# A hybrid encoder layer on one core: other places for evacuated tiles, more steps in the preparation of the scan's time steps, an earlier end of the descending scan, and narrower additions in the last blocks

## The chip, the cores and the metric

The kernel runs on 1 core of one Trainium2 chip. The metric is the device time of one execution in microseconds (us). Before the change the median of 3 runs is 1773.84 us (1771.46 to 1775.32).

Engines are named as in the profile: PE is TensorE (PEld its loading of weights), ACT ScalarE, DVE VectorE, POOL GpSimd, SP SyncE, which issues nearly all DMA transfers of this kernel.

## The reference

One layer of a bidirectional encoder for two request groups with shared weights, 1024 rows and 256 rows, that is 10 tiles of 128 rows:

```python
hn = rms_norm(x, norm_g)
proj = hn @ w_in                       # 2048 -> 4896 columns
xbc, z_ssd, dt_raw, q, k, v, z_att, mq, z_mem = split_cols(proj, IN_SIZES)
xbc = silu(centred_dwconv(xbc, conv_w, conv_b))
dt = softplus(dt_raw + dt_bias)
y = ssd_scan(forward) + ssd_scan(backward) + d_skip * xs
o_ssd = rms_norm(y * silu(z_ssd), ssd_norm_g)            # 1024 columns, two groups
o_att = window_attention(q, k, v, sink) * silu(z_att)    # 512 columns
o_mem = softmax_attention(mq, mem) * silu(z_mem)         # 512 columns
return x + concat([o_ssd, o_att, o_mem]) @ w_out
```

Everything is float32. `ssd_scan` is a chunked state-space scan in chunks of 128 rows; its weights are exponentials of cumulative sums of dt, and the kernel works with logarithms of dt.

## The kernel before, in words

Every weight product is done with split operands: a float32 matrix is split into a high and a low part (`wh`, `wl` for weights, `xH`, `xL` for activations), and three matmuls (`wh*xH`, `wl*xH`, `wh*xL`) stand for one. `wh` is made by ACT (L216), `wl` by DVE (L217), `xH` by ACT (L200) and `xL` by DVE (L201), the last two from a loaded tile `chd` of 128x640. The program runs through three parts: projection blocks whose features are worked through in pairs (L1316 to L1318), ordinary projection blocks (tokens by features, L268 to L270, and features by tokens, L303 to L305), and the output product, first two column blocks by L268 to L270, then eight units of pairs (`block_pair` with `ev_pair`), which end the program. PE's accumulators are five PSUM buffers (`acc`); all other products share three PSUM buffers (`mix`).

Beside the blocks of the projections and of the output product run two lanes of generators. After each step of a block, `pump` takes so many steps from each lane as the rates say; a step ends where the generator has a `yield`. Lane 0 has attention (`attn`, `mem_attn`), lane 1 the scan: `dt_prep` (time steps, cumulative sums and logarithms for one group of five tiles), `ssd_up` (ascending direction, tiles 0 to 9) and `ssd_down` (descending, tiles 7 to 0, then 9 and 8). So a `yield` more or less moves all later steps of a lane against the matmuls of the block. The framework then orders each engine's queue by priorities, and each engine works through its own queue in order.

The places that the change touches:

- `ev_gate` (L315) and `ev_raw` (L335) take a finished accumulator of a q, mq, z0 or z1 block to memory: ACT writes it into a tile of the pool `ev`, tag `evu` for even i and `evt` for odd i, two buffers each, and SP stores it (L342). A block of five tiles has i = 0 to 4. `base` is 0 for the first group of tiles and 5 for the second. The tag `ch` (four buffers of 128x640, `CH` = 4) is that of the loads `chd` and of the rows `yt` to which the output is added.
- `dt_prep` (L568): after the cumulative sums (`pacs`, copied to `ac` by ACT, L612) two rounds of Newton's method for the logarithm (ACT L614, DVE L616 to L620), then two exponentials (L621, L622), and, behind a `yield`, two transposes `pact` on PE (L629, L630), whose copy `acT` is stored.
- `ssd_up` (L876) pauses for some lane steps after its loads: 6 in tile 0, 8 in tile 4, otherwise 3.
- `ssd_down` (L1091): for tiles 0 and 8 (the last of each descending run) it pauses, calls `norm_ssd` (DVE L1074, scales `yd` by `yrs`, which POOL makes) and `turn_ssd` for both groups: four transposes `pr` each on PE (L647, the line of a helper), a copy `so` on ACT (L1088) and a store `oT<-so` on SP (L1089). For tile 0 the output product's first two column blocks wait for these stores: the last chd loads of the activations (`chd<-oT`, L188) read what they write.
- `mem_attn`, which runs beside this end: `pms` (scores, PE L811 to L813), row maxima `mm` (DVE L815), `mpr` (exponentials, ACT L821), `pmt` (transposes, PE L647), `mpT` (ACT L839), `pmo` (PE L850). Of `ssd_up` for tile 8: `pcb` (PE L893), `cb` (ACT L900), `pxs` (PE L930), `xs` and `xf` (DVE), `fh` (ACT L952), `pst` (PE L937).
- `ev_pair` (L1232) adds, for the eight units of the end, the seven products of a pair (p is the product's number) to two rows of tiles `r0` and `r1`, 128x640 each as two halves of 320; every `add` is DVE's L1240. `r0` is stored whole at p = 3 (L1256), `r1` in halves at p = 7 (L1259) and p = 4 (L1262), in this order at the end.

Of the kernel before, what the change touches and what calls it, by code (L numbers as in the profile page):

```python
# [19 lines left out]
P = 128  # L20
# [24 lines left out]
def hymba_encoder_kernel(  # L45
# [80 lines left out]
    def hv(ap, n=8):  # L126
        return ap.rearrange("p (h d) -> p h d", h=n)
# [184 lines left out]
            evac(1, ps[1])  # L312


    def ev_gate(c, base):  # L315
        def f(i, ps):
            z = ev.tile([P, 512], F32, tag="evt" if i % 2 else "evu", name="zs")
            A.activation(z, ps, AF.Tanh, scale=0.5)
            V.scalar_tensor_tensor(out=z, in0=z, scalar=1.0, in1=ps, op0=ALU.add, op1=ALU.mult)
            S.dma_start(z_d[c][base + i], z)  # L320
        return f
# [12 lines left out]

    def ev_raw(dst, base):  # L335
        def f(i, ps):
            if base == 0 and i > 2:
                z = fin.tile([P, 512], F32, tag="tH7" if i == 4 else "tL7", name="qs")
            else:
                z = ev.tile([P, 512], F32, tag="evt" if i % 2 else "evu", name="qs")  # L340
            last_raw[0] = A.activation(z, ps, AF.Copy).ins
            S.dma_start(dst[base + i], z)  # L342
        return f
# [224 lines left out]
    def dt_prep(t0):  # L568
        grp = t0 // 5
        ts = slice(t0, t0 + 5)  # L570
        flat = lambda a: a[:, ts, :].rearrange("p t h -> p (t h)")
        t6 = (t0 + 1) % 6
        wj, dd = [a[:, t6:t6 + 5, :].rearrange("p t h -> p (t h)") for a in (wj_all, dd_all)]
        t5 = lambda a: a.rearrange("p (t h) -> p t h", t=5)
        x = flat(dt_all)
        e, s = [mp.tile([P, 512], F32, tag="xs", name=n, bufs=2)[:, :160] for n in "es"]
        w, l = [mp.tile([P, 512], F32, tag=f"ya{i}", name=n, bufs=1)[:, :160] for i, n in enumerate("wl")]
        V.scalar_tensor_tensor(out=e, in0=x, scalar=-1.0, in1=x, op0=ALU.mult, op1=ALU.min)
        A.activation(e, e, AF.Exp)
        V.tensor_scalar(out=s, in0=e, scalar1=2.0, scalar2=None, op0=ALU.add)  # L580
        V.reciprocal(out=s, in_=s)
        V.tensor_mul(s, s, e)
        V.tensor_mul(w, s, s)
        V.tensor_scalar(out=e, in0=w, scalar1=1.0 / 17, scalar2=None, op0=ALU.mult)
        for c in (15, 13, 11, 9, 7, 5, 3):
            V.scalar_tensor_tensor(out=e, in0=e, scalar=1.0 / c, in1=w, op0=ALU.add, op1=ALU.mult)
        V.scalar_tensor_tensor(out=e, in0=e, scalar=1.0, in1=s, op0=ALU.add, op1=ALU.mult)
        V.tensor_scalar(out=e, in0=e, scalar1=2.0, scalar2=None, op0=ALU.mult)
        V.scalar_tensor_tensor(out=x, in0=x, scalar=0.0, in1=e, op0=ALU.max, op1=ALU.add)
        yield  # L590

        da = e
        V.tensor_mul(t5(da), dt_all[:, ts, :], aneg.unsqueeze(1).broadcast_to([P, 5, 32]))
        yield

        V.tensor_scalar(out=w, in0=x, scalar1=1e-30, scalar2=None, op0=ALU.max)
        V.tensor_scalar(out=l, in0=w.bitcast(I32), scalar1=math.log(2.0) / 2 ** 23, scalar2=-126.957 * math.log(2.0),
                        op0=ALU.mult, op1=ALU.add)
        yield
        yield  # L600
        lower = w2("lower")[:, :P]
        G.affine_select(out=lower, in_=ones, compare_op=ALU.is_ge, fill=0.0, base=0,
                        pattern=[[-1, P]], channel_multiplier=1)
        yield
        yield
        ps = psum("pacs")
        p5 = t5(ps[:, :160])
        T.matmul(p5[:, :, 0:16], upper, t5(da)[:, :, 0:16], start=True, stop=True)
        T.matmul(p5[:, :, 16:32], lower, t5(da)[:, :, 16:32], start=True, stop=True)
        T.matmul(ps[:, 160:320], ones, da, start=True, stop=True)  # L610
        ac = wb("ac", shape=(P, 512))
        A.activation(ac[:, :320], ps[:, :320], AF.Copy)  # L612
        for _ in range(2):
            A.activation(s, l, AF.Exp)  # L614
            d = da
            V.tensor_sub(d, w, s)  # L616
            V.tensor_add(s, w, s)
            V.reciprocal(out=s, in_=s)
            V.tensor_mul(d, d, s)
            V.scalar_tensor_tensor(out=l, in0=d, scalar=2.0, in1=l, op0=ALU.mult, op1=ALU.add)  # L620
        A.activation(flat(eacs_all), ac[:, 0:160], AF.Exp)  # L621
        A.activation(flat(cd_all), ac[:, 160:320], AF.Exp)  # L622
        V.tensor_sub(wj, l, ac[:, 0:160])
        V.tensor_add(dd, wj, ac[:, 160:320])
        A.activation(dd, dd, AF.Exp)
        V.tensor_sub(t5(wj)[:, :, 16:32], t5(wj)[:, :, 16:32], t5(wj)[:, :, 0:16])
        yield
        ps = psum("pact")
        T.transpose(ps[:, :P], ac[:, 0:128], ident)  # L629
        T.transpose(ps[:32, P:2 * P], ac[:, 128:160], ident)  # L630
        acT = wb("acT", shape=(P, 512))
        A.activation(acT[:, :P], ps[:, :P], AF.Copy)
        A.activation(acT[:32, P:2 * P], ps[:32, P:2 * P], AF.Copy)
        S.dma_start(ac_d[grp][0:P, :], acT[:, :P])
        S.dma_start(ac_d[grp][P:160, :], acT[:32, P:2 * P])
        yield
# [239 lines left out]
    def ssd_up(t):  # L876
# [7 lines left out]
        for g in range(2):  # L884
            x = wb("xc", F32R, shape=(P, 4, P))
            S.dma_start(x.bitcast(F32), xbc_d[4 * g:4 * g + 4, :, tok].rearrange("f p c -> p f c"))
            xc.append(x)
        for _ in range(6 if t == 0 else 8 if t == 4 else 3):
            yield

        ps = psum("pcb")
# [199 lines left out]
    def ssd_down(t):  # L1091
# [66 lines left out]
        last_y["y"] = t, [x[0] for x in ld], rs  # L1158
        yield
        if first:  # L1160
            for _ in range(3):
                yield
            norm_ssd()
            yield
            yield
            for g in range(2):
                turn_ssd(g)
                yield

# [60 lines left out]
    def ev_pair(u):  # L1232
# [6 lines left out]
        def add(out, ps, x):  # L1239
            V.tensor_tensor(out=out, in0=ps, in1=x, op=ALU.add)  # L1240

        def f(p, ps):
            if p == 1:
                A.activation(w[:, 0], ps, AF.Copy)
                add(r0[:, 0], ps, r0[:, 0])
            elif p == 2:
                add(r0[:, 0], ps, r0[:, 0])
            elif p == 6:
                add(w[:, 0], ps, w[:, 0])
            elif p == 5:  # L1250
                add(w[:, 1], ps, w[:, 0])
                add(r0[:, 1], w[:, 1], r0[:, 1])
                add(r1, w, r1)
            elif p == 3:
                add(r0[:, 1], ps, r0[:, 1])
                S.dma_start(hv(y_turned[rows_[0], :], 2), r0)  # L1256
            elif p == 7:
                add(r1, ps.unsqueeze(1).broadcast_to([P, 2, 320]), r1)
                S.dma_start(y_turned[rows_[1], 320:], r1[:, 1])  # L1259
            else:  # L1260
                add(r1[:, 0], ps, r1[:, 0])
                S.dma_start(y_turned[rows_[1], :320], r1[:, 0])  # L1262
# [546 lines left out]
```

## Time and profile before

| what | value |
|---|---|
| median of 3 runs | 1773.84 us |
| the profiled execution's own time | 1773.66 us |
| its span in the trace | 1772.0 us |
| PE's granted clock | 1.000 |
| DMA, mean over the span | 170 GB/s, 301.16 MB |

The span runs from the first instruction to the last; the execution's own time is a little longer. In a row of the timeline stand the start in us, the duration in us, the engine, the line, the operation, the tiles (out<-in), the count, and in brackets how long the engine stood idle before it and what ended that. Matmuls overlap: a 128x512 acc matmul is drawn 0.39 us long, and the next one starts 0.23 us later. SPq rows are issues of transfers and not their duration. In a row of the windows come busy times of PE, PEld, DVE, ACT and POOL with instruction counts, then the granted clock, the DMA share and GB/s.

### The profile page before, as it was taken

The page shows a single profiled execution, that of the slowest core. Times are in us where ns is not written, and L with a number is a line of the kernel's source. Part 1 is how long each engine was busy: PE and PEld are TensorE (multiplying, and loading weights), DVE is VectorE, ACT ScalarE, POOL GpSimd, SP SyncE. Part 2 cuts the span into 40 slices and gives each one's busy share as a digit, 9 for nine tenths or more (in the row PEclk, how much of TensorE's full clock was granted, in tenths as well). Part 3 has the DMA queues.
Part 4 walks back from the last instruction along what each step waited for, and adds up shares of the span by engine and source line. Part 5 has one row for each costly group of instructions (what it writes and reads, how often), then busy time and mean ns, then how long its engine had stood idle before and what let it go on. Part 6 is the DMA issues. An engine that isn't in the chain of part 4 may idle for free. (4 is left out here: it accounts for less than half of the span.)

```text
span 1772.0 us, 31942 instructions
## 1 busy us (share of the span) xinstructions
PE 1762.2 (99%) x11044; PEld 1608.4 (91%) x11044; DVE 1246.0 (70%) x2351; ACT 901.6 (51%) x2010; POOL 555.6 (31%) x980
## 2 busy tenths in 40 slices
PE   9999999999999999999999999999999999999999
PEld 7889999999998999999889988888988888899999
DVE  5596788888868878878665676566776654766665
ACT  6555455554434756656454555544446533543332
POOL 0105899998810100001001000011110000058775
PEclk9999999999999999999999999999999999999999
DMA  9654444445446645454545645557777755744442
GB/s 308 189 182 130 136 151 146 144 140 169 124 140 209 197 134 151 140 153 122 186 121 173 201 149 161 172 161 249 225 246 226 257 188 148 218 142 148 145 144 77
DMA packets 208210, 301.16 MB, mean 170 GB/s; under 512 B 19568, under 2 KB 86192, under 8 KB 208048
## 3 DMA queue, kind: packets, MB, share of 16 engines
q1 hardware_dynamic: 207904, 299.06, 54.1%
q8 instruction: 87, 1.43, 0.3%
q14 instruction: 75, 0.61, 0.1%
q10 hardware_dynamic: 144, 0.06, 0.0%
HBM read 236.36 MB, written 62.69 MB: 169 GB/s over the span
## 5 line engine op out<-in xcount | busy, mean ns | idle before, releaser
L217 DVE TENSOR_TENSOR wl<-wraw,wh 128x512 fp32r<-128x512 f32 (+1 forms) x480 | 346.4, 724 | 238.4 <-ACT wh L216 225.4
L216 ACT ACTIVATE wh<-wraw 128x512 fp32r<-128x512 f32 (+1 forms) x480 | 292.2, 613 | 301.6 <-PE acc L270 154.6
L268 PE MATMUL acc<-wh,xH 128*128 128x512 f32 (+1 forms) x1088 | 418.1, 385 | 0.0
L270 PE MATMUL acc<-wh,xL 128*128 128x512 f32 (+1 forms) x1088 | 410.4, 377 | 0.0
L269 PE MATMUL acc<-wl,xH 128*128 128x512 f32 (+1 forms) x1088 | 409.5, 376 | 0.0
L270 PEld LDWEIGHTS acc<-wh,xL 128*128 128x128 f32 x1088 | 204.2, 188 | 37.0 <-issue 0.2
L268 PEld LDWEIGHTS acc<-wh,xH 128*128 128x128 f32 x1088 | 204.3, 188 | 36.5 <-issue 2.7
L269 PEld LDWEIGHTS acc<-wl,xH 128*128 128x128 f32 x1088 | 204.5, 188 | 35.0 <-issue 1.2
L303 PE MATMUL acc<-xH,wh 128*128 128x320 f32 x640 | 203.0, 317 | 0.0
L305 PE MATMUL acc<-xH,wl 128*128 128x320 f32 x640 | 198.8, 311 | 0.0
L304 PE MATMUL acc<-xL,wh 128*128 128x320 f32 x640 | 198.5, 310 | 0.0
L216 ACT ACTIVATE sh<-ws 128x384 fp32r<-128x384 f32 x176 | 91.4, 523 | 204.8 <-POOL ws L1284 111.2
L217 DVE TENSOR_TENSOR sl<-ws,sh 128x384 fp32r<-128x384 f32 x176 | 124.4, 710 | 98.3 <-ACT sh L216 96.0
L1284 POOL TENSOR_TENSOR ws<-wraw 128x128 f32<-128x128 f32 x176 | 113.8, 646 | 202.4 <-DMA wraw<-in_w_in_pairs_dram 90.5
L303 PEld LDWEIGHTS acc<-xH,wh 128*128 128x128 f32 x640 | 120.1, 188 | 2.9 <-issue 2.4
L304 PEld LDWEIGHTS acc<-xL,wh 128*128 128x128 f32 x640 | 120.2, 188 | 1.7 <-issue 1.4
L305 PEld LDWEIGHTS acc<-xH,wl 128*128 128x128 f32 x640 | 120.2, 188 | 1.0 <-issue 0.9
L1284 POOL TENSOR_TENSOR ws<-wraw,ws 128x128 f32<-128x128 f32 x176 | 116.5, 662 | 13.8
L1284 POOL TENSOR_TENSOR ws<-ws,wraw 128x128 f32<-128x128 f32 x176 | 118.2, 671 | 0.0
L1284 POOL TENSOR_TENSOR wraw<-wraw 128x128 f32<-128x128 f32 x176 | 111.5, 633 | 13.7
L654 POOL MEMSET lgw<- 128x1 f32 x40 | 4.2, 105 | 312.0 <-DVE lg L718 161.6
L377 DVE SCALAR_TENSOR_TENSOR c<-u,vec,c 128x638 f32<-128x638 f32 (+1 forms) x96 | 90.0, 939 | 1.1 <-ACT c L372 0.4
(442 smaller groups left out, 3931.1 us busy)
## 6 DMA issues: line engine op xcount, KB each, us to landing
wraw<-in_w_in_laid_dram SPq DMA_DIRECT2D x176, 256.0 KB, 2.9
wraw<-in_w_in_pairs_dram SPq DMA_DIRECT2D x112, 256.0 KB, 2.7
wraw<-in_w_out_laid_dram SPq DMA_DIRECT2D x64, 256.0 KB, 3.6
wraw<-in_w_out_pairs_dram SPq DMA_DIRECT2D x64, 256.0 KB, 2.7
rf<-ac SPq DMA_DIRECT2D x40, 256.0 KB, 4.0
rb<-ac SPq DMA_DIRECT2D x40, 256.0 KB, 4.7
wraw<-in_w_mem_laid_dram SPq DMA_DIRECT2D x32, 256.0 KB, 4.3
xst<-in_x_sample_dram SPq DMA_DIRECT2D x20, 256.0 KB, 5.3
```

Source lines behind the costliest of these rows:

```text
L216: a = A.activation(h, raw, AF.Copy)
L217: b = V.tensor_sub(l, raw, h.bitcast(F32))
L268: T.matmul(ps[t][:, :n], sh, h[:, :n], start=(k_ == 0), stop=False)
L269: T.matmul(ps[t][:, :n], sh, l[:, :n], start=False, stop=False)
L270: T.matmul(ps[t][:, :n], sl, h[:, :n], start=False, stop=(k_ == KT - 1))
L303: T.matmul(o, sh, cur["H", q][:, m, c], start=(k == 0), stop=False)
L304: T.matmul(o, sh, cur["L", q][:, m, c], start=False, stop=False)
L305: T.matmul(o, sl, cur["H", q][:, m, c], start=False, stop=(k == KT - 1))
L377: V.scalar_tensor_tensor(out=c[0], in0=u[:, k:k + n], scalar=cw[k], in1=c[0], op0=ALU.mult, op1=ALU.add)
L654: G.memset(w.bitcast(F32)[(slice(None),) + tuple(slice(n - 1, n) for n in shape)], 0.0)
L1284: G.tensor_tensor(out=o, in0=x, in1=y, op=op)
```

## The change

1. A helper `out_place` chooses the tile for `ev_gate` and `ev_raw`. For the second group of tiles (`base` 5), i = 3 and i = 4 go to the tag `ch`; for the first group all stays.
2. In `dt_prep` the two exponentials move ahead of the two rounds of the logarithm, and each round ends with a `yield`.
3. The pauses of `ssd_up` for tiles 0 and 4 are two lane steps shorter.
4. In `ssd_down`, for tile 0: the pause ahead of `norm_ssd` is one step shorter, one `yield` behind it goes, and that between the two `turn_ssd` goes.
5. In `ev_pair` the store of `r0` is split in two halves (p = 2 and p = 3), and the addition of `w` to `r1`, 640 wide at p = 5, becomes two of 320 (p = 6 and p = 5).

```diff
+    def out_place(i, base, name):
+
+        if i > 2 and base == 0 and name == "qs":
+            return fin.tile([P, 512], F32, tag="tH7" if i == 4 else "tL7", name=name)
+        if i > 2 and base:
+            return rp.tile([P, 640], F32, tag="ch", name=name, bufs=CH)[:, :512]
+        return ev.tile([P, 512], F32, tag="evt" if i % 2 else "evu", name=name)
...
-            z = ev.tile([P, 512], F32, tag="evt" if i % 2 else "evu", name="zs")
+            z = out_place(i, base, "zs")
...
-            if base == 0 and i > 2:
-                z = fin.tile([P, 512], F32, tag="tH7" if i == 4 else "tL7", name="qs")
-            else:
-                z = ev.tile([P, 512], F32, tag="evt" if i % 2 else "evu", name="qs")
+            z = out_place(i, base, "qs")
...
         A.activation(ac[:, :320], ps[:, :320], AF.Copy)
+        A.activation(flat(eacs_all), ac[:, 0:160], AF.Exp)
+        A.activation(flat(cd_all), ac[:, 160:320], AF.Exp)
         for _ in range(2):
             A.activation(s, l, AF.Exp)
...
             V.scalar_tensor_tensor(out=l, in0=d, scalar=2.0, in1=l, op0=ALU.mult, op1=ALU.add)
-        A.activation(flat(eacs_all), ac[:, 0:160], AF.Exp)
-        A.activation(flat(cd_all), ac[:, 160:320], AF.Exp)
+            yield
...
-        for _ in range(6 if t == 0 else 8 if t == 4 else 3):
+        for _ in range(4 if t == 0 else 6 if t == 4 else 3):
             yield
...
         if first:
-            for _ in range(3):
+            for _ in range(2 if t == 0 else 3):
                 yield
             norm_ssd()
             yield
-            yield
+            if t:
+                yield
             for g in range(2):
                 turn_ssd(g)
-                yield
+                if t or g:
+                    yield
...
             elif p == 2:
                 add(r0[:, 0], ps, r0[:, 0])
+                S.dma_start(y_turned[rows_[0], :320], r0[:, 0])
             elif p == 6:
                 add(w[:, 0], ps, w[:, 0])
+                add(r1[:, 0], w[:, 0], r1[:, 0])
             elif p == 5:
                 add(w[:, 1], ps, w[:, 0])
                 add(r0[:, 1], w[:, 1], r0[:, 1])
-                add(r1, w, r1)
+                add(r1[:, 1], w[:, 1], r1[:, 1])
             elif p == 3:
                 add(r0[:, 1], ps, r0[:, 1])
-                S.dma_start(hv(y_turned[rows_[0], :], 2), r0)
+                S.dma_start(y_turned[rows_[0], 320:], r0[:, 1])
```

What this does to the order of the engines is shown at three places. The first is PE at the end of the descending scan, at about 1318 us of the span. The `acc` matmuls are those of the first output block; the number of an `acc` is that of a tile of 128 rows, five to a round. Before:

```order
L268 MATMUL acc_16123<-wh_16158,xH0_15840 128x512
L269 MATMUL acc_16123<-wl_16159,xH0_15840 128x512
L270 MATMUL acc_16123<-wh_16158,xL0_15841 128x512
L647 MATMUL pr_16179<-identr_84,yw_16177 128x128 x4
L647 MATMUL pr_16189<-identr_84,yw_16187 128x128 x4
L783 MATMUL pmq_16199<-identr_84,mq_16145 128x128 x4
```

And with the change (the helper's line is L653 there, and acc_16121 to acc_16125 are the five tiles):

```order
L268 MATMUL acc_16121<-wh_16178,xH0_15840 128x512
L269 MATMUL acc_16121<-wl_16179,xH0_15840 128x512
L270 MATMUL acc_16121<-wh_16178,xL0_15841 128x512
L653 MATMUL pr_16151<-identr_84,yw_16149 128x128 x4
L653 MATMUL pr_16161<-identr_84,yw_16159 128x128 x4
L268 MATMUL acc_16122<-wh_16178,xH0_15840 128x512
```

The eight transposes stood behind the last of the five tiles of a round and now stand behind the first: 12 matmuls earlier. pmq keeps its place behind the round.

The second is ACT just after it. chd_16197, 16237, 16324 and 16365 are the loads of one stretch of activations, chd_16424 and later ones those of the next. Before:

```order
L796 ACTIVATE mqh_16204<-pmq_16199 128x512
L216 ACTIVATE wh_16403<-wraw_16401 128x512
L821 ACTIVATE mpr_16250,mden_16251<-pms_16240,mm_16247,mr_16153 128x256 x2
L900 ACTIVATE cb_16266<-pcb_16257 128x256
L821 ACTIVATE mpr_16278,mden_16279<-pms_16268,mm_16275,mr_16153 128x256 x2
L200 ACTIVATE xH2_16320<-chd_16197,vec_200 128x640
L200 ACTIVATE xH2_16320<-chd_16237,vec_200 128x640
L216 ACTIVATE wh_16450<-wraw_16448 128x512
L200 ACTIVATE xH2_16320<-chd_16324,vec_200 128x640
L200 ACTIVATE xH2_16320<-chd_16365,vec_200 128x640
L952 ACTIVATE fh_16340<-xf_16338 128x512
```

And with the change; behind the last row shown come one more wh and then fh_16340:

```order
L802 ACTIVATE mqh_16204<-pmq_16199 128x512
L200 ACTIVATE xH2_16320<-chd_16197,vec_200 128x640
L216 ACTIVATE wh_16403<-wraw_16401 128x512
L200 ACTIVATE xH2_16320<-chd_16237,vec_200 128x640
L200 ACTIVATE xH2_16320<-chd_16324,vec_200 128x640
L200 ACTIVATE xH2_16320<-chd_16365,vec_200 128x640
L827 ACTIVATE mpr_16250,mden_16251<-pms_16240,mm_16247,mr_16173 128x256 x2
L906 ACTIVATE cb_16266<-pcb_16257 128x256
L200 ACTIVATE xH3_16505<-chd_16424,vec_200 128x640
L827 ACTIVATE mpr_16278,mden_16279<-pms_16268,mm_16275,mr_16173 128x256 x2
L216 ACTIVATE wh_16450<-wraw_16448 128x512
L200 ACTIVATE xH3_16505<-chd_16471,vec_200 128x640
```

The four xH of the first stretch stood behind both softmax steps (mpr) and now stand ahead of them; the first two of the next stretch stand ahead of fh, behind which they were.

The third is PE in the second `dt_prep`, at about 875 us, beside a step of `mem_attn`. Before:

```order
L647 MATMUL pmt<-identr,mprw 128x128 x4
L629 MATMUL pact<-identr,ac 128x128
L630 MATMUL pact<-identr,ac 32x128
L850 MATMUL pmo<-mpT,mv 128x128 x8
L268 MATMUL acc<-wh,xH_6939 128x512
```

And with the change (lines L653, L856, L635 and L636 there):

```order
L653 MATMUL pmt<-identr,mprw 128x128 x4
L856 MATMUL pmo<-mpT,mv 128x128 x8
L635 MATMUL pact<-identr,ac 128x128
L636 MATMUL pact<-identr,ac 32x128
L268 MATMUL acc<-wh,xH_6939 128x512
```

The two transposes pact stood ahead of pmo and now stand behind it.

## Prediction

> **What bounds the kernel now.** I read the head of the page first, then the list of waits on TensorE, then the timeline of each place that the change touches. The head gives the span and how much of it TensorE is busy:
>
> ```profile
> span 1772.0 us, 31942 instructions
> PE 1762.2 (99%) x11044; PEld 1608.4 (91%) x11044; DVE 1246.0 (70%) x2351; ACT 901.6 (51%) x2010; POOL 555.6 (31%) x980
> ```
>
> TensorE works for 1762.2 of 1772.0 us, and the change leaves its matmuls as they are, so only its waits can be won or lost. All of them, by what ended them (total us, times, longest):
>
> ```profile
> PE warm L1592 <- DVE zero L1590: 1.3, 1, 1.3
> PE pst L937 <- ACT fh L952: 1.1, 1, 1.1
> PE pmt L647 <- DVE mpr L827: 1.1, 1, 1.1
> PE ppt L647 <- ACT pT L734: 1.0, 1, 1.0
> PE pmo L850 <- ACT mpT L839: 0.8, 1, 0.8
> PE pr L647 <- ACT so L1088: 0.4, 1, 0.4
> PE acc L1318 <- DVE wl L217: 0.3, 1, 0.3
> ```
>
> They come to 6.0 us, 0.34% of the span. The edits lie near three of them (ppt, pmo, pst) and at the end of the program, after TensorE's last matmul. So 1.0 + 0.8 + 1.1 us and some tenths at the end are all that can be won; against the 0.2% (3.5 us) that a measurement of this kernel can tell from no change, a gain can hardly be seen. A loss has no such bound.
>
> **The new places for evacuated tiles: -0.95.** TensorE, ScalarE and SyncE where mq is stored:
>
> ```profile
> 1228.12 0.65 PE L647 MATMUL ppt<-identr,lgw 128*128 128x128 f32 x4 [0.95 <-ACT pT L734]
> 1227.20 0.60 ACT L341 ACTIVATE qs<-acc 128x512 f32<-128x512 f32 x1 [1.06 <-DMA mq<-qs]
> 1221.72 1.31 SPq L342 DMA_DIRECT2D mq<-qs  x2
> ```
>
> The fifth evacuation of the mq block (i = 4) stands 1.06 us on ScalarE, since its evu buffer is free only when the store of i = 0, issued at 1221.72, is done. pT is queued behind it on ScalarE, and TensorE waits 0.95 us for pT. With i = 3 and 4 in ch buffers no store is waited for: -0.95. At worst half comes back, if a ch buffer is still being read.
>
> The price is in the same queue. Four chd<-oT loads (320 KB each) for the output blocks, which SyncE issued two projection blocks earlier, now come at 1232 to 1246, because the ch buffers are lent out until then:
>
> ```profile
> 1232.00:1246.00 14.00, 14.00 (x113) 12.71 (x111) 10.18 (x19) 4.96 (x11) 5.46 (x12) 1.00 0.94 294
> ```
>
> The DMA share there is 0.94 already, so some transfers land later, by an estimated 0.4 to 1.1 us. TensorE is busy for all 14 us of that stretch, and the next wait behind it (pr for so, 0.4) hangs on a VectorE chain that doesn't start with these transfers. I take 0, and up to +0.7 if that chain is late.
>
> **A yield in each round of the logarithms: +0.25.** The second dt_prep, on TensorE and ScalarE:
>
> ```profile
> 875.21 0.30 PE L629 MATMUL pact<-identr,ac 128*128 128x128 f32 x1
> 875.46 1.06 PE L850 MATMUL pmo<-mpT,mv 128*128 128x128 f32 x8
> 877.30 1.16 PE L850 MATMUL pmo<-mpT,mv 128*128 128x128 f32 x8 [0.79 <-ACT mpT L839]
> 875.91 0.34 ACT L614 ACTIVATE s<-l 128x160 f32<-128x160 f32 x1 [2.05 <-DVE l L620]
> 876.67 0.58 ACT L839 ACTIVATE mpT<-pmt 128x512 f32<-128x512 f32 x1
> ```
>
> ScalarE stands 2.05 us before s, in order, and mpT comes behind; both keep their places in ScalarE's queue. So pmo still starts at 877.30. But the two pact transposes, which took 875.21 to 875.46 ahead of pmo, now follow it: they lay within the wait and now lie on the path. +0.25, at best 0 (if mpT comes earlier), at most +0.3. In the first dt_prep no wait of TensorE is near, and the scan tiles' pauses, shorter by as many steps as dt_prep has more, leave TensorE's order alone: 0, and what hides them is the matmuls of the projection block.
>
> **The shorter descending end: +1.7.** First the transposes pr, which move ahead of 12 acc matmuls:
>
> ```profile
> 1315.85 0.39 PE L268 MATMUL acc<-wh,xH 128*128 128x512 f32 x1
> 1318.58 0.80 PE L647 MATMUL pr<-identr,yw 128*128 128x128 f32 x8
> 1316.36 0.88 DVE L1074 TENSOR_SCALAR yd<-yd,yrs 128x512 f32<-128x512 f32 x2 [2.16 <-POOL yrs L1157]
> 1316.96 0.49 POOL L1082 MEMSET yw<- 128x1 f32 x2 [0.64 <-DVE yd L1074]
> 1319.36 1.07 ACT L1088 ACTIVATE so<-pr 128x512 f32<-128x512 f32 x2
> ```
>
> The 12 acc take 2.73 us (0.2275 each), so TensorE now reaches pr at 1315.85. Its input, the first half of the yd pair, is ready at about 1316.8 (1317.2 if it needs the memset too): a new wait of 1.1 us (1.0 to 1.4), where there was none. In return the stores oT<-so leave earlier: pr at 1316.95, so from 1317.45 to 1318.0, the store at 1318.05 and not at 1319.97 as in the next rows (the chain of waits, the windows, then the timelines):
>
> ```profile
> 1319.97 4.54 DMA oT<-so
> 1324.90 5.86 DMA chd<-oT
> 1318.00:1322.00 4.00, 4.00 (x27) 3.42 (x26) 1.39 (x2) 2.10 (x4) 0.00 (x0) 1.00 0.94 287
> 1324.53 1.75 SPq L188 DMA_DIRECT2D chd<-oT  x4
> 1325.78 0.57 ACT L821 ACTIVATE mpr<-pms,mm,mr 128x256 f32<-128x256 f32 x1 [1.84 <-DVE mm L817]
> 1328.65 0.83 ACT L200 ACTIVATE xH<-chd,vec 128x640 fp32r<-128x640 f32 x1 [0.31 <-DMA chd<-oT]
> 1330.79 0.83 ACT L200 ACTIVATE xH<-chd,vec 128x640 fp32r<-128x640 f32 x1 [1.29 <-DMA chd<-oT]
> 1331.52 0.61 ACT L216 ACTIVATE wh<-wraw 128x512 fp32r<-128x512 f32 x1
> 1332.04 1.54 ACT L200 ACTIVATE xH<-chd,vec 128x640 fp32r<-128x640 f32 x2
> 1334.10 0.63 ACT L952 ACTIVATE fh<-xf 128x512 fp32r<-128x512 f32 x1 [0.52 <-DVE xf L950]
> 1327.03 0.54 PE L930 MATMUL pxs<-identr,xc 128*128 128x128 f32 x4
> 1334.78 0.50 PE L937 MATMUL pst<-fh,bth 128*128 128x512 f32 x1 [1.09 <-ACT fh L952]
> ```
>
> Before, ScalarE ran the first softmax mpr at 1325.78 and only then came to xH, which waited for the loads. Now four xH stand ahead of the first mpr and two more ahead of fh; each waits for its own chd load, and all that is behind waits with it. Worked through: the store lands 3.6 us after 1318.05 (4.54 before; two wraw loads that lay ahead of it now come after the loads), so the loads are issued from 1321.65. The first is there 4.1 us later (1324.53 to 1328.65), at 1325.8; the fourth between 1328.2 (0.8 apart) and 1329.9 (before, the fourth xH began by 1332.8, 8.3 after the first issue): I take 1329.0. Then xH 0.75 and two mpr, 0.57 each: 1330.9. pxs needs the PSUM buffer that mpr frees (three serve all of these tiles); it stands 5 acc later than before and behind the pr wait, at 1327.03 + 1.14 + 1.1 = 1329.3. So it waits 1.6 us (0.8 to 2.5).
>
> Next pst. It stands three acc later; without its own wait it would start at 1334.78 - 1.09 + 0.68 = 1334.37, and with the two new ones at 1337.1. The fifth load can't be issued before the first chd buffer is read, about 1.6 us after it landed, 1327.4; it lands after 4.1 to 5.9 us, 1331.5 to 1333.3. xH (0.73), the second mpr (1.1), wh (0.52), xH, wh, and fh (0.68 from its start to pst) come to 4.3 us: 1335.8 to 1337.6. So fh is about even with TensorE, and I give it 0.1. New waits 1.1 + 1.6 + 0.1, less the old 1.1: +1.7, bounds 0 and +3. The two wraw loads that SyncE now issues behind five chd loads are wanted only at about 1342, so nobody waits for them.
>
> **The pairs' additions and the split store: -0.3.** The end of the program, after TensorE's last matmul:
>
> ```profile
> 1768.04 0.31 PE L1318 MATMUL accm<-rH,wl 128*128 128x320 f32 x1
> 1766.68 0.82 DVE L1240 TENSOR_TENSOR yr<-yu,yr 128x640 f32<-128x640 f32 x1
> 1767.42 0.48 DVE L1240 TENSOR_TENSOR yr<-acc,yr 128x320 f32<-128x320 f32 x1
> 1767.82 0.81 DVE L1240 TENSOR_TENSOR yr<-accm,yr 128x640 f32<-128x640 f32 x1
> 1768.74 0.49 DVE L1240 TENSOR_TENSOR yr<-accm,yr 128x320 f32<-128x320 f32 x1
> ```
>
> VectorE runs these four additions without a gap worth the name, and the last store is issued behind the last of them. The first becomes 320 wide (0.48 for 0.82, the other half having been added at p = 6), so all that follows could come 0.34 sooner; but the last one needs TensorE's last result, there at 1768.35, and then starts at about 1768.45 for 1768.74: -0.3 (0 to -0.35). In the seven earlier units each half store and each addition lies beside matmuls that wait for neither: 0. Their price without that cover would be the 0.48 of an addition.
>
> **Sum.** -0.95 + 0.25 + 1.7 - 0.3 = +0.7 us. The profiled execution took 1773.66 us by its own time (1772.0 of span, 1.66 around it) and lies 0.18 below the median of the runs, 1773.84. So it would take 1774.4 after, and the median goes to 1774.5.
>
> **Rivals.**
>
> *The loads land early (0.2).* For it: the moved store and its loads meet two wraw transfers less. If store and loads take some 2.9 us each (below what the rows have), the loads are there from 1323.9 to 1325.2, before mm at about 1325.7 gives ScalarE its first mpr; xH then costs the softmax nothing, pxs finds its buffer, and fh is early. The stretch then has the new 1.1 for the old 1.1: 0, and the sum is -0.95 + 0.25 - 0.3 = -1.0: 1772.8. Against it: 4.54 and 5.86 in the chain, under a DMA share of 0.94. Beside this stands a rule of the Trainium skill, "DMA: Bandwidth & Descriptors", section "Anatomy of one DMA — SWDGE (gpsimd) path", which puts a transfer at about 2.0 us plus its bytes over 436 GB/s (given there for transfers that GpSimd issues). By that a store of 256 KB would be estimated at 2.6 us and a load of 320 KB at 2.75, the loads would be there in time, and this rival would be the result. The two chain rows speak against it by 1.9 and 3.1 us: the rule holds no time in which a transfer stands behind others.
>
> *The loads land late, and the softmax and fh with them (0.14; slower).* One mechanism: ScalarE, in order, behind the xH that waits for the fifth and sixth load. If the store takes 4.54 as before and each load 5.86, the first is there at 1318.05 + 4.54 + 5.86 = 1328.45; the fifth, issued 1.6 later, at 1335.9; then 4.3 us as above, and 0.4 for a sixth load that comes behind, give pst at 1340.6 for 1337.2. That is 3.4 more than the forecast: 1777.9. It decides from pst at 1340.0 on, where the loss passes 3.5 us. For it: SyncE has seven loads in a row here. Against: two of them, the wraw pair, now come after.
>
> *The places do nothing (0.02).* The wait at 1228 goes over to another store or to pT's own input: the 0.95 is not won, 1775.5.
>
> **How the numbers follow.** The forecast as worked out has 0.56, and 0.08 is for what none of these cases names, half to each side. The forecast's bounds are -0.7 (the stretch at 0) and +2.0 (the stretch at 3), that is 1773.1 to 1775.9. Early loads take the range down to 1772.8, and with pr's new wait hidden as well to 1771.7; of the late loads it takes in the part up to 1777.4. So 1771.7 to 1777.4, with the last end of the late loads and what the trace can't show left out. Faster by over 0.2% (under 1770.3) would need more than all the waits named above: 0.04, the half of what no case names. Slower by over 0.2% (over 1777.4): the greater part of the late loads, 0.09, and the other half of the unnamed, 0.04 (the loads moved to 1232 come to mind): 0.13. Within 0.2%: 0.83.
>
> **What the next profile would show.** Right: no wait of ppt for pT, and qs without a DMA wait; pmo's wait larger by 0.25; a new wait of pr for yd near 1 us; a wait of pxs for mpr; xH ahead of mpr with DMA waits on ScalarE; the last store issued 0.3 sooner after TensorE's last matmul. Wrong: mpr that starts before 1326.5 or so by before's time line (early loads); pst that starts over 5 us later against the matmuls around it (late loads); or a wait of TensorE in a place that isn't named here, above all from 1232 to 1252.

## The result and the profile after

After the change the median is 1775.68 us of 21 runs (1774.35 to 1778.87), beside 1772.78 us of 21 runs of the kernel before (1770.06 to 1775.32): a ratio of 1.0019, 95% interval 1.0013 to 1.0025, that is +3.4 us (2.3 to 4.4). (The ratio is an estimate from the runs and not the quotient of the two medians, which lie 2.9 us apart.) The profiled execution took 1776.19 us, 2.5 more than that of before. The head of its page:

```profile
span 1774.5 us, 31954 instructions
PE 1763.5 (99%) x11044; PEld 1608.9 (91%) x11044; DVE 1248.1 (70%) x2359; ACT 901.7 (51%) x2010; POOL 557.4 (31%) x980
```

TensorE still runs the same 11044 matmuls and is busy for 99%. The list of its waits (total us, times, longest):

```profile
PE pxs L936 <- ACT mpr L827: 1.8, 1, 1.8
PE warm L1602 <- DVE zero L1600: 1.3, 1, 1.3
PE pr L653 <- DVE yd L1080: 1.0, 1, 1.0
PE pmo L856 <- ACT mpT L845: 0.8, 1, 0.8
PE pk L559 <- DVE kh L553: 0.8, 1, 0.8
PE pd L1128 <- DMA ydT<-yd: 0.7, 1, 0.7
PE acc L1328 <- DVE wl L217: 0.7, 2, 0.4
PE pmt L653 <- DVE mpr L833: 0.2, 1, 0.2
PE pst L944 <- DVE fl L966: 0.2, 1, 0.2
```

The wait of ppt for pT (0.95) and that of pst for fh (1.1) are gone; pxs and pr are new; pk and pd are two that the prediction did not name, and pd, at 1245.92, lies in the stretch from 1232 to 1252 where its list counts a wait that is not named as a sign of being wrong. The places of these waits, in TensorE's timeline:

```profile
578.41 0.37 PE L559 MATMUL pk<-identr,kh 128*128 128x128 f32 x2 [0.76 <-DVE kh L553]
879.07 1.16 PE L856 MATMUL pmo<-mpT,mv 128*128 128x128 f32 x8 [0.80 <-ACT mpT L845]
880.07 0.27 PE L635 MATMUL pact<-identr,ac 128*128 128x128 f32 x1
1245.92 0.52 PE L1128 MATMUL pd<-identr,ydT 128*128 128x128 f32 x4 [0.67 <-DMA ydT<-yd]
1318.02 0.84 PE L653 MATMUL pr<-identr,yw 128*128 128x128 f32 x8 [0.97 <-DVE yd L1080]
1332.31 0.54 PE L936 MATMUL pxs<-identr,xc 128*128 128x128 f32 x4 [1.79 <-ACT mpr L827]
```

In ScalarE's timeline at the end of the descending scan, the first softmax step mpr stands behind four xH:

```profile
1326.85 0.83 ACT L200 ACTIVATE xH<-chd,vec 128x640 fp32r<-128x640 f32 x1 [3.98 <-DMA chd<-oT]
1328.76 2.40 ACT L200 ACTIVATE xH<-chd,vec 128x640 fp32r<-128x640 f32 x3 [0.56 <-DMA chd<-oT]
1331.07 0.55 ACT L827 ACTIVATE mpr<-pms,mm,mr 128x256 f32<-128x256 f32 x1
1337.80 0.61 ACT L958 ACTIVATE fh<-xf 128x512 fp32r<-128x512 f32 x1
```

The engine stood 3.98 us ahead of the first xH, for a chd load, and only when the fourth xH was done did the first mpr start, at 1331.07; fh was early enough, since pst behind it waited for nothing on ScalarE. The issues on SyncE that belong to it:

```profile
1319.19 1.21 SPq L1095 DMA_DIRECT2D oT<-so  x2
1323.46 1.74 SPq L188 DMA_DIRECT2D chd<-oT  x4
```

And the end of the program, on VectorE, TensorE and SyncE:

```profile
1770.35 1.41 DVE L1248 TENSOR_TENSOR yr<-accm,yr 128x640 f32<-128x640 f32 x2
1770.86 0.31 PE L1328 MATMUL accm<-rH,wl 128*128 128x320 f32 x1
1771.79 0.33 SPq L1272 DMA_DIRECT2D out_dram<-yr  x1
```

TensorE's last matmul ends at 1771.17, and the span ends 3.30 us later; before it was 3.60 (1768.35 to 1771.95).

Laid beside the trace of before, instruction by instruction, TensorE of the two profiled executions drifts apart so (start of the named matmul after, less its start before, us):

| at (us of before) | matmul | later by |
|---|---|---|
| 508.89 | prx, ahead of all edits | 1.24 |
| 846.37 | pmt, behind the first dt_prep | 1.94 |
| 875.46 | the first pmo, beside the second dt_prep | 1.68 |
| 885.17 | pmq, behind pmo and pact | 1.93 |
| 1228.12 | ppt, at the new places | 0.76 |
| 1244.41 | pd, behind its new wait | 1.51 |
| 1287.16 | ppt, ahead of the end of the scan | 1.02 |
| 1339.31 | pmo, behind the end of the scan | 2.72 |

By this single pair the end costs 1.70, as forecast. But 1.24 us were lost ahead of the first edit, where TensorE runs the same matmuls in the same order in both kernels. One pair of traces therefore cannot size these terms, and the experiments had to.

### The profile page after: what moved, and what is told of

Its sections match the earlier page's. It is cut to its first block, busy times and chain, and to the rows that moved or that the text cites. A ratio compares the mean times of both kernels' runs of the same rounds, so it can differ in the third digit from the quotient of the medians.

```text
span 1774.5 us, 31954 instructions
## 1 busy us (share of the span) xinstructions
PE 1763.5 (99%) x11044; PEld 1608.9 (91%) x11044; DVE 1248.1 (70%) x2359; ACT 901.7 (51%) x2010; POOL 557.4 (31%) x980
## 4 chain that ended last, share of the span: by engine, by line
PE 95%; DVE 2%; DMA 1%; issue 0%; ACT 0%; SPq 0%; POOL 0%; DVEq 0%; ACTq 0%
PE acc L268 13%; PE acc L270 12%; PE acc L269 12%; PE acc L1328 7%; PE acc L1326 7%; PE acc L1327 7%; PE acc L303 5%; PE acc L305 5%; PE acc L304 5%; PE accm L1327 3%; PE accm L1326 3%; PE accm L1328 3%; PE po L750 1%; PE py L1020 1%; PE pmo L856 1%; PE ppt L653 1%
```

## The experiments

The theory at the start: the loss is at the descending end, by ScalarE's order (xH, which waits for the loads, ahead of a softmax step that is ready). The rivals: the steps of `dt_prep` cost more than the 0.25 given to them, or the moved loads at 1232 do.

**The parts one by one.** Four kernels, each timed against before: the end alone (part 4 of the change), the steps alone (2 and 3), places and additions alone (1 and 5), and the kernel before once more.

The end alone:

```diff
-            for _ in range(3):
+            for _ in range(2 if t == 0 else 3):
                 yield
             norm_ssd()
             yield
-            yield
+            if t:
+                yield
...
                 turn_ssd(g)
-                yield
+                if t or g:
+                    yield
```

> The kernel before with the earlier end of the descending scan alone (the pause, the two yields of ssd_down for tile 0). Theory: the loss of this part is what the trace after shows from pr to pst, a wait of pr for yd near 1.0, one of pxs for mpr near 1.8, and pst's old wait of 1.1 gone; TensorE comes out of the stretch 1.8 us later, ratio 1.0010 (+1.8 us). Rival: the stretch's loss came from transfers that the other parts moved into it (the chd loads of the first output block, the rf and rb loads); then pxs waits under 0.5 here and the ratio is 1.0000 to 1.0003.

Measured: ratio 1.0016 (1.0007 to 1.0025), +2.8 us. TensorE's two longest waits in this part, in its list:

```profile
PE pxs L930 <- ACT mpr L821: 2.5, 1, 2.5
PE pr L647 <- DVE yd L1074: 1.0, 1, 1.0
```

The mechanism is there with nothing else changed, and here it costs more than in the trace of after. The windows of this kernel behind the wait show what comes with it (PE busy and its count first; behind POOL the granted clock, the DMA share and GB/s):

```profile
1326.00:1332.00 6.00, 3.52 (x19) 2.66 (x18) 3.87 (x8) 4.74 (x10) 0.00 (x0) 1.00 0.85 261
1332.00:1334.00 2.00, 2.00 (x13) 1.68 (x14) 2.00 (x8) 2.00 (x6) 0.10 (x1) 0.81 0.96 291
1334.00:1336.00 2.00, 2.00 (x6) 1.63 (x5) 2.00 (x8) 1.09 (x4) 0.10 (x1) 0.50 0.74 237
1336.00:1338.00 2.00, 2.00 (x9) 1.55 (x9) 1.72 (x3) 0.36 (x1) 0.00 (x0) 0.84 1.03 357
1338.00:1340.00 2.00, 2.00 (x14) 1.50 (x13) 0.88 (x2) 1.54 (x4) 0.00 (x0) 1.00 0.79 256
```

A busy TensorE is granted half its clock: 6 matmuls stand in the third window, where the last has 14. The rows of its timeline that begin and end this:

```profile
1331.92 0.53 PE L930 MATMUL pxs<-identr,xc 128*128 128x128 f32 x4 [2.48 <-ACT mpr L821]
1333.11 0.65 PE L268 MATMUL acc<-wh,xH 128*128 128x512 f32 x1
1336.53 0.46 PE L270 MATMUL acc<-wh,xL 128*128 128x512 f32 x1
1336.83 0.40 PE L268 MATMUL acc<-wh,xH 128*128 128x512 f32 x1
```

From 1333.11 to 1336.53 eight acc intervals take 3.42 us, 0.43 each; at the usual 0.2275 they take 1.82. The wait of 2.48 us so costs another 1.6. In the trace of after the wait was 1.79, and the clock stayed at 1.00 behind it.

Every run has its mean granted clock on record, and one such stretch takes 0.001 off it. It is under 1.000 in 9 of the 11 runs of the end alone, in 8 of the 21 of after and in 6 of the 33 of before that were timed beside the end alone. But the clock is the smaller part of the loss: the 13 runs of after at 1.000 have a median of 1775.38 us, still 2.9 above the 1772.47 of the 27 such runs of before.

The steps alone:

```diff
+        A.activation(flat(eacs_all), ac[:, 0:160], AF.Exp)
+        A.activation(flat(cd_all), ac[:, 160:320], AF.Exp)
         for _ in range(2):
...
-        A.activation(flat(eacs_all), ac[:, 0:160], AF.Exp)
-        A.activation(flat(cd_all), ac[:, 160:320], AF.Exp)
+            yield
...
-        for _ in range(6 if t == 0 else 8 if t == 4 else 3):
+        for _ in range(4 if t == 0 else 6 if t == 4 else 3):
```

> The kernel before with the part of dt_prep alone (exponentials ahead, a yield in each round, the two shorter pauses of ssd_up). Theory: the first dt_prep, which the prediction put at 0, costs 1.3 us near 575 (pst for fl, pk for kh), since its rf and rb loads go out 4 to 5 us later and the chd loads behind them land late; some 0.7 of it is won back at 844, where VectorE bounds; +0.2 in the second dt_prep. In sum +0.8, ratio 1.0005. Rival: the waits near 575 are scatter of one execution; then no wait of pk here, and the ratio is 1.0001 (+0.2 us).

Measured: 1.0011 (1.0002 to 1.002), +2.0 us, where the prediction had 0.25 and the expectation 0.8. The 11 runs fall into two groups, five from 1772.5 to 1773.7 and six from 1775.5 to 1777.0; the profiled one (1773.00) is of the lower, so no trace here shows what the upper group pays for.

Places and additions alone:

```diff
+        if i > 2 and base:
+            return rp.tile([P, 640], F32, tag="ch", name=name, bufs=CH)[:, :512]
...
+                add(r1[:, 0], w[:, 0], r1[:, 0])
...
-                add(r1, w, r1)
+                add(r1[:, 1], w[:, 1], r1[:, 1])
```

> The kernel before with the new places (out_place) and the narrower additions with the split store. Theory: no wait of ppt for pT, -1.0; pd for ydT waits 0.7 and the wait of pr behind it shrinks by 0.5, +0.25; the end -0.3. In sum -1.1, ratio 0.9994. Rival: the loads moved to 1232 cost as much as the places win; then the ratio is 0.9998 to 1.0003 with pd's wait over 1.2.

Measured: 0.9996 (0.9987 to 1.0005): -0.7 us, not told apart from nothing. No loss by the moved loads at 1232 shows.

The kernel before again, nothing edited:

> The kernel before, once more, for the scatter of one execution's trace against another's with the same order of instructions. Theory: the 1.0 to 1.4 us by which the kernel after is late before 545 us, where the orders of the two agree almost row for row, is scatter of transfers (the start: 0.65; the pair units: 0.7); then this copy too shows steps of 0.3 to 0.7 against the profile of before ahead of 545, of either sign, and the ratio is 1.0000. Rival: it is a cost of the change, and the copy lies within 0.2 of the profile of before all along.

Measured: 1.0002 (0.9993 to 1.0011). TensorE's waits in the profile of this second execution, from its list:

```profile
PE pst L937 <- ACT fh L952: 1.2, 2, 0.9
PE acc L1318 <- DVE wl L217: 0.9, 2, 0.6
PE pk L554 <- DVE kh L548: 0.7, 1, 0.7
PE pmo L850 <- ACT mpT L839: 0.7, 1, 0.7
PE pr L647 <- ACT so L1088: 0.5, 1, 0.5
PE pmt L647 <- DVE mpr L827: 0.3, 1, 0.3
```

The same program has no wait of ppt for pT here, and it has the wait of pk that looked new after the change. Waits of this size come and go between executions. The three parts sum to 2.8 + 2.0 - 0.7 = 4.1 us, beside 3.4 for the whole.

**Is it ScalarE's order?** After, with the output product's xH (L200, from chd) held behind the second softmax step of tile 5 in ScalarE's queue:

```diff
-                A.activation(pr[:, j * 256:(j + 1) * 256], ps[:, j * 256:(j + 1) * 256], AF.Exp,
+                soft[t, hp] = A.activation(pr[:, j * 256:(j + 1) * 256], ps[:, j * 256:(j + 1) * 256], AF.Exp,
...
-            A.activation(h, ch, AF.Copy, scale=gain)
+            with ExitStack() as st:
+                if (5, 1) in soft:
+                    st.enter_context(tc.issue_after(soft[5, 1]))
+                A.activation(h, ch, AF.Copy, scale=gain)
```

> The kernel after, with xH on ScalarE kept behind the second softmax step of mem_attn (an edge in issue order; stores, loads and pr stay as early as in the kernel after). Theory: the loss lies in pxs, which waits for mpr behind four xH; without that pxs finds its buffer, fh comes early because the loads do, and of the stretch only pr's 1.0 is left, against the old wait of pst: time near that of before, ratio 1.0000 to 1.0005. Rival: the early loads crowd the transfers, or the early pr itself is the loss; then the ratio stays at 1.0012 or above.

Measured: 1.0003 (0.9994 to 1.0012), where after has 1.0019 (1.0013 to 1.0025): the intervals do not meet. From TensorE's list of waits:

```profile
PE pr L657 <- DVE yd L1084: 1.1, 1, 1.1
PE pst L947 <- ACT fh L962: 0.2, 1, 0.2
```

and from ScalarE's timeline:

```profile
1325.61 0.57 ACT L831 ACTIVATE mpr<-pms,mm,mr 128x256 f32<-128x256 f32 x1 [1.84 <-DVE mm L827]
1328.06 1.56 ACT L204 ACTIVATE xH<-chd,vec 128x640 fp32r<-128x640 f32 x2
```

mpr now waits for its own input alone, xH follows without a wait, pxs finds its buffer, and fh is still in time. The wait of pxs was the order's doing, not that of the transfers: the first four chd loads landed no sooner here, 4.6 to 5.7 us after their issue, against 3.4 to 5.5 in the trace of after. The same edge with the end alone (before, part 4, and the edge):

```diff
+                if (5, 1) in soft:
+                    st.enter_context(tc.issue_after(soft[5, 1]))
```

> The kernel before with the earlier end alone and xH kept behind the softmax. Theory: pr waits 1.0, pxs nothing, pst under 0.5; ratio 1.0003 (1.0000 to 1.0006) where the earlier end alone had 1.0016, and no stretch of half clock on TensorE. Rival (the wait of pr, or the transfers): ratio over 1.0010.

Measured: 1.0005 (0.9996 to 1.0014) for 1.0016 (1.0007 to 1.0025) without the edge; the intervals overlap. The trace has no wait of pxs and no half clock at this place, and all 11 runs have a mean clock of 1.000, where 9 of 11 were below it without the edge.

**Does a longer wait bring the half clock to the changed kernel?** After, with two more exponentials, of which nothing is used, ahead of the first softmax row of tile 5:

```diff
+            for _ in range(2 if t == 5 and hp == 0 else 0):
+                A.activation(pr[:, 0:256], ps[:, 0:256], AF.Exp, scale=r[:, 0:1], bias=m[:, 0:1])
```

> The kernel after with two more exponentials on ScalarE ahead of the first softmax row (results written over by the right ones), so that pxs waits about 1.0 longer, near 2.9. Theory: an idle time of TensorE of about 2.5 us or more takes its clock to half for some 3.4 us behind it, which adds 1.6 us to the wait (seen once, in the earlier end alone, with a wait of 2.48; not seen after 1.79): here the granted clock is about 0.5 for 3 us behind pxs. Rival: the half clock there came by chance and not from the wait; then the granted clock stays at 1.00 here.

Measured: one time, 1778.75 us. The wait of pxs from TensorE's list, and two windows behind it:

```profile
PE pxs L938 <- ACT cb L908: 2.9, 1, 2.9
```

```profile
1334.00:1336.00 2.00, 2.00 (x12) 1.60 (x11) 2.00 (x9) 2.00 (x8) 0.00 (x0) 0.56 0.93 275
1336.00:1338.00 2.00, 2.00 (x7) 1.57 (x7) 2.00 (x8) 1.93 (x4) 0.10 (x1) 0.59 0.95 299
```

The wait now ends with cb, which is right behind mpr. With 1.1 us more of it the clock fell in the place where the trace of after kept it.

**After without one part.** Without the steps (the diff of the steps, reversed):

```diff
-            yield
+        A.activation(flat(eacs_all), ac[:, 0:160], AF.Exp)
+        A.activation(flat(cd_all), ac[:, 160:320], AF.Exp)
...
-        for _ in range(4 if t == 0 else 6 if t == 4 else 3):
+        for _ in range(6 if t == 0 else 8 if t == 4 else 3):
```

> The kernel after without the part of dt_prep (exponentials, yields, pauses as before). Theory by the time of the steps alone (1.0011): this part costs 1 to 2 us on its own, and the ratio falls to 1.0010 or less. Rival, by the traces (they show 0.2 for it and nothing else): the ratio is 1.0017 to 1.0020.

Measured: 1.0013 (1.0004 to 1.0022), between the theory and its rival; the interval holds both, so this run does not settle what the steps cost. Its list of waits has the longest wait of pxs of all, and the clock fell behind it (0.52 from 1334 to 1336):

```profile
PE pxs L935 <- ACT mpr L826: 3.2, 1, 3.2
```

Without the end (the diff of the end, reversed):

```diff
-            for _ in range(2 if t == 0 else 3):
+            for _ in range(3):
...
-                if t or g:
-                    yield
+                yield
```

> The kernel after with the end of the descending scan as before. Theory: the end costs 1.7 us in its waits and 1.6 more in each execution whose pxs wait takes the clock to half; without it the rest is the steps (+1.2 by the traces' mean), the places (0 to -0.4) and the end of the program (-0.3): ratio 1.0003 (1.0000 to 1.0007), no pxs wait over 0.5, no half clock there. Rival: the parts hinder one another and the end alone is not the loss; then 1.0010 or above.

Measured: 1.0003 (0.9994 to 1.0012). The end is worth some 2.8 us here too. Yet the one profiled execution of this kernel has a long wait in the old order as well, in its list and in a window behind it:

```profile
PE pst L943 <- ACT fh L958: 3.0, 2, 2.3
```

```profile
1338.00:1340.00 2.00, 2.00 (x6) 1.55 (x5) 1.89 (x4) 1.79 (x4) 0.00 (x0) 0.50 0.87 273
```

A wait of 2.32 us for fh, and half clock: the old end is not free of it either. It meets it more seldom: the mean clock is under 1.000 in 2 of the 11 runs here.

**Yields or pauses?** The shorter pauses alone:

```diff
-        for _ in range(6 if t == 0 else 8 if t == 4 else 3):
+        for _ in range(4 if t == 0 else 6 if t == 4 else 3):
```

> The kernel before with the pauses of ssd_up for tiles 0 and 4 two steps shorter, and no yield in dt_prep. Theory: what costs in the steps' part is that SyncE issues the rf and rb loads late, close ahead of the chd loads; with the pause alone they come as early as before or earlier, and TensorE gains or loses nothing between 545 and 880 us beyond scatter (from -0.8 to +0.8 in the kernels with the old steps): ratio 1.0000 (0.9996 to 1.0004). Rival: the shorter pause is the cost; then 1.0006 or above and over +0.9 in that stretch.

Measured: 1.0021 (1.0012 to 1.003), +3.7 us, where 1.0000 was expected. Its two longest waits:

```profile
PE pst L937 <- ACT fh L952: 2.8, 1, 2.8
PE pst L938 <- DVE fl L960: 1.6, 1, 1.6
```

The first is the old end's wait for fh, at 1338.90, with half clock behind it; this execution, at 1779.38, is the slowest of the 11. The second, at 573.19, lies in the first `dt_prep`'s stretch. From pacs to the last pmo, 545 to 880, TensorE takes 336.0 us here, 2.3 above the mean of the old form (the table below). So both signs of the rival came. The theory of the late loads missed: SyncE issues the first rf load at 551.12, in the profile of before at 551.43.

The exponentials and yields alone:

```diff
+        A.activation(flat(eacs_all), ac[:, 0:160], AF.Exp)
+        A.activation(flat(cd_all), ac[:, 160:320], AF.Exp)
...
+            yield
```

> The kernel before with the exponentials ahead and a yield in each round, the pauses of ssd_up as before. Theory: the rf and rb loads go out later still than with both edits, so the waits near 575 stay or grow: +0.9 or more between 545 and 880, +0.2 of it by pact behind pmo; ratio 1.0006 (1.0003 to 1.0012). Rival: the yields themselves are free; then 1.0001.

Measured: 1.0034 (1.0021 to 1.0048), +6.0 us over five runs, above the expected range. The same stretch takes 335.8 us, 2.1 more than the old form. The longest wait, from its list, and the windows around it:

```profile
PE pst L939 <- DVE fl L961: 2.8, 2, 2.6
```

```profile
590.00:592.00 2.00, 0.00 (x0) 0.00 (x0) 2.00 (x4) 2.00 (x6) 0.00 (x0) 1.00 0.81 278
592.00:594.00 2.00, 1.81 (x11) 1.74 (x12) 2.00 (x6) 1.92 (x5) 0.00 (x0) 1.00 0.77 245
```

Each half of the edit moves the scan's lane by two steps against the projection blocks, and that alone measured more than both together (1.0011): 3.7 and 6.0 against 2.0, though for the pauses the two intervals overlap. So the costs of the halves do not add up. That what costs is where the lane then stands, and that the two shifts largely cancel, is a reading and not shown.

**The parts that are worth it.** Before with places, additions, the new end and the edge, `dt_prep` and pauses as before:

```diff
+                if (5, 1) in soft:
+                    st.enter_context(tc.issue_after(soft[5, 1]))
...
+                if t or g:
+                    yield
```

> The kernel before with the new places, the narrower additions and the earlier end, xH kept behind the softmax, and dt_prep as before: what the runs leave as harmless or good. Theory: places 0 to -0.4, the end of the program -0.3, the stretch at the end of the scan +0.5 (pr 1.0 against pst's old wait): -0.2, ratio 0.9999 (0.9995 to 1.0003). Rival: the early end has a price of its own in transfers: 1.0005 or above.

Measured: 0.9996 (0.9987 to 1.0005), median 1771.91. It is faster than the changed kernel; against the kernel before no difference can be told.

**The 14 traces together.** Distances on TensorE from one start to another, in us, the mean and the extremes over the profiles of before, after and the experiments:

| stretch | old form | new form |
|---|---|---|
| first dt_prep (pacs, about 544) to the last pmo before pact (878): steps | 333.67 (333.23 to 334.79), 7 traces | 334.53 (333.91 to 335.20), 5 traces |
| pr (1285) to the last pmo (1341): end | 56.27 (54.32 to 59.14), 7 traces | 59.38 (57.60 to 60.67), 3 traces |
| the same with the edge of mpr ahead of xH | | 56.36 (56.04 to 56.59), 3 traces |
| wait of ppt at 1228: places | 0.5 (0 to 1.23), 7 traces | 0, 7 traces |
| wait of pd at 1245 for ydT: places | 0, 7 traces | 0.4 (0 to 0.75), 7 traces |
| last matmul's end to the end of the span: additions | 3.60 to 3.62, 7 traces | 3.30 to 3.32, 7 traces |

The stretches of the two kernels with half a step edit and of the one with added exponentials are left out where that edit bears on them. (A later pd, at 1283 to 1286, waited 1.0 in one trace of the old places and 1.1 in one of the new.) By these means the change should cost +0.9 and +0.2 for pact (steps), +3.1 (end), -0.5 and at most +0.2 (places) and -0.3 (additions): 3.4 to 3.6 us, beside 3.4 measured. So close an agreement is in part luck: the first two rows scatter by more than 1 us, two of the three new ends and two of the seven old ones have the half clock, and timed alone the steps gave 2.0 and not 1.1.

## Why the prediction was half right

It forecast +0.7 us, and with a chance of 0.83 a change within 0.2%; +3.4 (2.3 to 4.4) was measured, 0.19%. The time of 1775.68 lies 1.2 above the forecast 1774.5 and within its range, but that the change, five times as large as forecast, stayed within 0.2% is close to luck. The terms that were not put at 0 came out with the right sign; the sizes of the end, the first dt_prep and the places did not.

- **The end, +1.7: the mechanism held, the size failed at the step that took one wait for one price.** In the trace of after the chain is as worked out: pr waited 0.97 for 1.1, the first xH began at 1326.85 (1325.8 on before's clock, as forecast), pxs waited 1.79 for 1.6, pst not at all for fh. Behind this agreement two errors cancelled: the store took 4.3 us from its issue to the loads' issue (forecast 3.6) and the first load 3.4 (forecast 4.1). But over three traces with the new end and nothing added the wait of pxs was 1.79, 2.48 and 3.23, and the sum had no term for TensorE's clock: behind 2.48 and 3.23 it ran at half speed, for 1.6 us more in the trace where it was worked out. By the runs at 1.000 the clock is the smaller part of the loss. The mean of the stretch is +3.1. Since the edge on ScalarE takes the stretch back to 56.36 and the time back to 1.0003, the cause is shown: work that waits for a DMA, ahead of work that is ready, on an engine that takes its queue in order.
- **The clock.** Waits of 1.09 and 1.79 us left it at 1.00; behind 2.32, 2.48, 2.79, 2.87 and 3.23 us it was about half, for 3.41 us. One wait of 2.58 us, at 592, left it at 1.00, so a length alone doesn't decide. The traces tell what does: in all 14 the record of the granted clock changes only at whole multiples of 3.41 us from its first entry, and half clock followed where TensorE had stood idle for 1.69, 2.09, 2.32, 2.69 and 2.87 us in all within one such step. No other step before the program's end had more than 1.57 us. Of the steps in which the last matmul ends, those with 1.65 and 1.79 us stayed at full, and those with 2.00 and more did not. So the border lies near 1.7 us in a step (the profile models the ends of matmuls, so it is no sharper), and the place of a wait counts: the 2.58 fell on two steps as 1.30 and 1.28, and the 1.79 of after as 0.75 and 1.04, which was its luck. Beside this stands a rule of the Trainium skill, "TensorE: Matmul & The Clock Gate", section "HAM oscillation — how this bites in real kernels", that TensorE should have no idle gap above some 3.4 us; by it none of these waits, and no term of the sum, would have cost clock. The traces speak against it: five gaps below 3.4 us did.
- **The first dt_prep, 0: failed.** The step "the pauses, shorter by as many steps as dt_prep has more, leave TensorE's order alone" was right of TensorE's order and wrong of the time. The store of the cumulative sums leaves later, and the scan's loads of them with it: SyncE issues the first rf load at 556.09 after, and at 551.43 and 553.80 in the two traces of before. The stretch up to the last pmo is longer by 0.9 us in the mean, with a scatter of over 1 us in each kind, and the timed kernel with the steps alone gives +2.0 (0.4 to 3.5). What causes it stays open. The late loads are argued from their place only, and the run with the shorter pauses alone speaks against them as the whole cause: there the loads are as early as before, and the stretch is longer by 2.3.
- **The second dt_prep, +0.25: right.** pmo waited 0.80 for 0.79 in the trace of after, and pact follows it, in every trace with both edits of the steps, for 0.2 (0.25 in the table of drifts, 1.68 to 1.93). (The list of what to look for said that pmo's wait would grow by 0.25; the wait stayed and pact came behind it, as the working had it.)
- **The places, -0.95: too much.** The wait is gone in all seven traces with the new places, but it was there in only four of seven with the old ones. The mean gain is 0.5. Timed with the additions, the places gave -0.7 us where these terms had -1.25, not told apart from nothing. The price, put at 0 and up to +0.7, shows as the wait of pd for ydT, 0.67 in the trace of after, in the stretch that was named; most of it is won back at the next pr (the drift falls from 1.51 to 1.02 by 1287).
- **The additions, -0.3: right**, 0.30 in every trace.
- **The rivals.** The loads did not land early: 3.4 us for the first load of after and 4.3 for the store, against some 2.9 in that rival. By the estimate from the Trainium skill, "DMA: Bandwidth & Descriptors", section "Anatomy of one DMA — SWDGE (gpsimd) path" (2.6 and 2.75 us), it would have been the result. Over the traces the store took 4.0 to 5.3 us and the first four loads 3.4 to 8.5. The late loads had the right place and half the right mechanism: ScalarE in order behind xH. It was the wait ahead of mpr that grew and brought the clock down, not that ahead of fh.

## What to carry to other kernels

A wait of about 1 us in one profile is a draw, not a price: take two profiles of the same kernel before a term is put at its full size, and see whether the profiled run is typical of its kernel's runs. Where an edit frees a transfer earlier, look at what its reader then stands in front of in an in-order queue; an edge that keeps ready work ahead cost nothing that could be measured here and gave 2.8 us back. And price a wait of TensorE above some 1.7 us with a chance of the half clock behind it, here 1.6 us more.

## What was not expected of the hardware

TensorE's granted clock went to half behind single gaps of 2.3 to 3.2 us in a kernel that is busy for 99%, for 3.41 us at a time, and once did not behind 2.58 us, which fell across two steps of its clock record. And two executions of the same program drift apart by most of a microsecond ahead of any edit: 0.88 us at 508.89 between the two profiles of before.
